# Entry into attention: query operands made earlier, searches held back, masks ranked last

## The chip, the cores and the metric

The kernel runs on one core of a Trainium2 chip. The metric is the device time of one launch in microseconds (us), the median of several runs. Five engines work in parallel, each through its own queue in order: TensorE (PE, the matrix multiplier; its weight loads are PEld), VectorE (DVE), ScalarE (ACT), GpSimd (POOL) and SyncE (SP), which here issues the loads and stores (DMA). An instruction that waits for an operand holds everything behind it on its engine. Matrix products go to PSUM, a small memory with eight banks; the rest lies in SBUF. The clock of TensorE is granted by a throttle and falls to half in some stretches; the profile shows it.

## What is computed

A decoder layer over 1024 tokens of width 1024. One projection of `h` gives queries, keys and values of 8 heads, the operands of a light indexer, and 512 pooling channels. The indexer scores every earlier token for every query; only the 256 best take part in the attention of that query. Then come an output projection, a layer norm and a gated feed-forward block with a second norm. What matters here:

```python
logits = einsum('bqhd,bsd->bqhs', iqb, ik) * (IDX_DIM ** -0.5)
score = einsum('bqh,bqhs->bqs', w, relu(logits))
score = where(causal, score, -inf)
_, idx = top_k(score, k_sel)              # k_sel = 256
...
s = einsum('bqhd,bqkhd->bhqk', qb, kg) * (HEAD_DIM ** -0.5)
p = softmax(where(valid, s, -inf))
o = einsum('bhqk,bqkhd->bqhd', p, vg)
```

## The kernel before, in words

**Tiles.** Tokens are cut into eight tiles of 128, numbered 0 to 7. Tile `i` sees `i + 1` tiles of keys, so tile 7 has scores of 128 x 1024 and tile 2 of 128 x 384. Tiles 0 and 1 see 256 tokens or fewer and need no selection. Matrix products are done in three passes of high and low parts, so an operand is a pair: ScalarE makes the high part by a copy and VectorE the low part by a subtraction.

**Searches and masks.** The 256th best score of each query is found by bisection on the bits of the score (`bisect`, lines 560 to 658): some first steps, 15 rounds over the upper half word, a middle step, 16 rounds over the lower one, then the mask, which overwrites the scores with a bias. A round counts with one instruction per tile how many scores lie above a candidate and updates the candidate with two short ones. Tiles 3 and the pair 5, 4 count on ScalarE (`TILES_A`, in `search_a`); tile 2 and the pair 7, 6 count on VectorE (`TILES_V`, in `search_v`). First steps, middle steps and masks of all of them run on VectorE. In the profile the search of 7 and 6 writes `junk_X` from `keysD_T`, that of 2 `junk_X` from `keysA_X` with `colsE_X`, that of 5 and 4 `junkA_T`, that of 3 `junkB_X`; `score_X` holds scores and, later, the masks.

**The planner.** While the program is written down, each queue (`Queue`, lines 131 to 183) keeps a modelled time with modelled costs (`cost`). Each search is a generator, a stream, that yields its next piece as (engine, cost) before it issues it. Whenever an instruction is about to be written and its operands are ready only later by the model, `fill` (line 693) is called: it looks for stream pieces of the same engine whose start plus cost fits before that time (with a small slack) and writes them first. Among those that fit it takes the one with the earliest start and, in a tie, one of ScalarE's streams (`st[3] not in TILES_A`); among equals the first in the list `streams` wins. The stream of tile 2 (`LATE`) gets nothing while the stream of 7 and 6 is unfinished. `need(i)` (line 689) writes all pieces that are left until the mask of tile `i` is issued. Where a queue's name is in `pinned`, the order written down is kept; elsewhere a scheduler may move independent instructions. `advance` pins the first piece of the stream of tile 2.

**Projections.** Lines 917 to 962 go over 24 groups `n_`: eight for the pooling channels, eight for keys (`k`, tile t), eight for values (`v`, tile t, groups 16 to 23). Work that follows a group, such as rotating and transposing a key tile (`k_transpose`) or taking a value tile into SBUF (`v_take`), is registered with `at_(slot, f)` and written behind the products of group `slot`. The queues of TensorE, VectorE, ScalarE and GpSimd are pinned here (and SP's).

**The entry.** Rotated queries lie in memory (`q_d`). Behind the last group, the queries of tiles 7 and 6 are loaded (`q_load`) and transposed by TensorE (`q_transpose`, four instructions each); what is left of the slots' work follows; then `q_make` writes `q_operands` for both: four ScalarE copies and two VectorE subtractions each. The operand of tile 7 lies in `qabh`, on the place of `hT`, that of tile 6 in `qabw[0]`, on the place of the projection weights `ws`, so neither can be written while the projections run.

**Attention.** 32 units, one for each group of two tiles `g` (3 first), pair of heads `pr` and tile `i`: tiles 7 and 6 alternate over four pairs, then 5 and 4, 3 and 2, 1 and 0. A unit has two score matrices (`u_scores`, tile `s`; PSUM holds those of one large unit at a time), the sum with the mask and the row maximum on VectorE, the exponential on ScalarE (`u_exp`, which calls `need(i)`), the division on GpSimd (`u_norm`), transposes on TensorE (`u_trans`, tile `pT`), and behind two tiles the product with the values (`pair_pv`, tile `o`) and its split (`pair_cat`). Scores run `AHEAD = 2` units ahead of the transposes. `Q_AT` places the query operands of the next group. Behind the last unit follow the output projection `wo` and the rest of the layer.

Of the kernel before, what the change touches and what calls it, by code (L numbers as in the profile page):

```python
# [12 lines left out]
F32R = mybir.dt.float32r  # L13
# [31 lines left out]
LATE = [2]  # L45
# [141 lines left out]
def decoder_layer_kernel(  # L187
# [84 lines left out]
    def raw_slot():  # L272
        n_raw[0] += 1
        return RAW[(n_raw[0] - 1) % 3]
# [280 lines left out]
    keys = {2: kA[:, 0:192], 3: kA[:, 192:448], 4: k4, 5: k5, 6: kD[:, 0:448], 7: kD[:, 448:960]}  # L555
    keys = {i: kw.bitcast(I16) for i, kw in keys.items()}

    biased = set()

    def bisect(tiles, cols, on_act):  # L560

# [9 lines left out]
        one = lambda c, m: c[:, m : m + 1]  # L571
        w_ = lambda i: (i + 1) / 8
        for m, i in enumerate(tiles):
            yield "V", 1.13 * w_(i)
            V.tensor_scalar(trash(i), score(i), 0.0, 0.0, ALU.is_ge, ALU.add, accum_out=one(cntc, m))
        yield "V", 0.6
        V.tensor_scalar(pr, cntc, float(TOPK), None, ALU.is_ge)
        V.tensor_scalar(sg, pr, 2.0, -1.0, ALU.mult, ALU.add)
        V.tensor_scalar(flip, pr, 32768.0, -32768.0, ALU.mult, ALU.add)
# [1 line left out]
            n = P * (i + 1)  # L581
            V.tensor_scalar(one(kp, m), one(pr, m), -float(2 * TOPK - 1 - n), -float(n - TOPK + 1), ALU.mult, ALU.add)
        for m, i in enumerate(tiles):
            yield "V", 1.1 * w_(i)

            hv = score(i).bitcast(I16).rearrange("p (n two) -> p n two", two=2)
            V.tensor_tensor(kv[i], hv[:, :, 1], one(flip, m).to_broadcast([P, P * (i + 1)]), ALU.bitwise_xor)
            if on_act:
                V.tensor_scalar(one(thr, m), one(kp, m), 2.0, float(P * (i + 1) + 1), ALU.mult, ALU.add)
        sum_w = sum(w_(i) for i in tiles)  # L590

        def search_v(bits, base, low):
            V.memset(cand, float(1 << (bits - 1)))
            for b in range(bits - 1, -1, -1):
                yield "V", 0.4 + 1.08 * sum_w + 0.35 * nt
                for m, i in enumerate(tiles):
                    dt = U16 if low else I16
                    V.tensor_scalar(trash(i).bitcast(dt), kv[i].bitcast(dt), one(cand, m), one(base, m),
                                    ALU.is_ge, ALU.add, accum_out=one(cntc, m))
                off = -float(1 << (b - 1)) if b > 0 else -1.0  # L600
                for m in range(nt):
                    V.tensor_scalar(one(pr, m), one(cntc, m), 0.0, float(1 << b), ALU.is_ge, ALU.mult)
                for m in range(nt):
                    V.tensor_scalar(one(cand, m), one(pr, m), one(cand, m), off, ALU.add, ALU.add)

        def search_a(bits, low):

            V.memset(cand, 0.5 - float(1 << (bits - 1)))
            for b in range(bits - 1, -1, -1):
                for m, i in enumerate(tiles):  # L610
                    yield "A", 0.9 * w_(i) + 0.45
                    A.activation(trash(i), kv[i].bitcast(U16 if low else I16), AF.Sign, bias=one(cand, m),
                                 accum_out=one(cntc, m))
                yield "A", 0.55 * nt

                for m in range(nt):
                    A.activation(one(pr, m), one(cntc, m), AF.Sign, bias=one(thr, m))
                for m in range(nt):
                    A.activation(one(cand, m), one(pr, m), AF.Identity, scale=-0.5 * float(1 << b), bias=one(cand, m))
            yield "V", 0.1  # L620
            V.tensor_scalar(cand, cand, -1.0, None, ALU.mult)

        yield from (search_a(15, False) if on_act else search_v(15, kp, False))
        V.tensor_copy(M, cand)
        for m, i in enumerate(tiles):
            yield "V", 1.8 * w_(i)
            V.tensor_scalar(trash(i).bitcast(I16), kv[i], one(M, m), one(kp, m), ALU.is_gt, ALU.add,
                            accum_out=one(ng, m))
            lv = score(i).bitcast(U16).rearrange("p (n two) -> p n two", two=2)
            V.scalar_tensor_tensor(kv[i].bitcast(U16), kv[i], one(M, m), lv[:, :, 0], ALU.is_equal, ALU.mult)  # L630
            if on_act:
                V.tensor_scalar(one(thr, m), one(ng, m), 2.0, float(P * (i + 1) + 1), ALU.mult, ALU.add)
# [31 lines left out]
    def open_stream(*a):  # L664
        pinned.update(PIN)
        b = bisect(*a)
        streams.insert(0, [T.t, next(b), b, a[0], True])
        times.fill = fill

    def start(st):  # L670
        return max(st[0], queues[st[1][0]].t)

    def advance(st):
        fill, times.fill = times.fill, None
        q = queues[st[1][0]]
        held = st[3] == LATE and st[4] and "V" not in pinned
        st[4] = False
        if held:
            pinned.add("V")
        try:  # L680
            st[1] = next(st[2])
        except StopIteration:
            streams.remove(st)
        st[0] = q.t
        if held:
            pinned.discard("V")
        times.fill = fill

    def need(i):
# [3 lines left out]
    def fill(q, until):  # L693
        while True:

            first = [st for st in streams if 7 in st[3]]
            todo = [st for st in streams if not (first and st[3] == LATE) and st[1][0] == q.name and start(st) + st[1][1] <= until + SLACK.get(q.name, 0.0)]
            if not todo:
                return
            advance(min(todo, key=lambda st: (start(st), st[3] not in TILES_A)))  # L700


    n_rr = [0]
# [209 lines left out]
    def take(t, pp, slot):  # L913
        raw = rope_pool(t, pp)
        at_(slot, lambda: k_transpose(t, raw))

    groups = [("u", g, c) for g in (3, 2, 1, 0) for c in range(2)] + [("k", t, 0) for t in range(NT)] + [("v", t, 0) for t in range(NT)]

    PAIRS = (0, 6, 8, 14, 16)
    held, pair = {}, None  # L920
    for n_, (kind, a, b) in enumerate(groups):
        if n_ in PAIRS:
            pb = psB("pair")
            held[n_], held[n_ + 1] = pb[:, 0:512], pb[:, 512:1024]
            pair = [(held[q_], u_f(*groups[q_][1:]) if kind == "u" else t_f(groups[q_][1])) for q_ in (n_, n_ + 1)]
        if n_ in held:
            for kp in range(2):
                for pp, f in pair:
                    f(pp, [4 * (n_ not in PAIRS) + 2 * kp, 4 * (n_ not in PAIRS) + 2 * kp + 1])
        else:  # L930
            held[n_] = psA("pj")
            (u_f(a, b) if kind == "u" else t_f(a))(held[n_], range(KT))
        pp = held[n_]
        if n_ in (2, 10):
            w_loads(wk_in if n_ == 2 else wv_in)
        if n_ in (7, 8, 15, 16):
            for kp in ((0, 1) if n_ % 2 else (2, 3)):
                w_split(kp)
        nd = n_ + 2 if n_ in PAIRS else n_ + 1
        if kind == "u":  # L940
            at_(nd, lambda a=a, b=b, pp=pp: u_take(a, b, pp))
            if b == 1:
                at_(nd + 1, lambda a=a: u_split(a))
                at_(nd + 1, lambda a=a: u_split2(a))
                at_(nd + POOL_AT, lambda a=a: u_pool(a))
        elif kind == "k":
            tr = n_ + (4 if n_ in PAIRS or n_ - 1 in PAIRS else 3)
            at_(nd, lambda a=a, pp=pp, tr=tr: take(a, pp, tr))
        else:
            at_(nd, lambda a=a, pp=pp: v_take(a, pp))  # L950
        if n_ == 20:
            SP.dma_start(GR, gate_d[0].to_broadcast([P, 1024]))
        q_ = n_ - MOD_AT
        if 0 <= q_ < 9:
            if q_:
                mod_fin(q_ - 1)
            if q_ < 8:
                mod_half(2 * q_)
        for f in late.pop(n_, []):
            f()  # L960
        if 0 <= q_ < 8:
            mod_half(2 * q_ + 1)
# [11 lines left out]

    ptb = [[buf("H", (2 * s_ + e) * 2048, 2048, "pT").rearrange("p (j q) -> p j q", j=8) for e in (0, 1)] for s_ in (0, 1)]
    smr = buf("H", 8192, 6144, "sm")
    qabh = buf("H", 14336, 1536, "qab", F32R)
    qabw = [buf("W", 2048 * i, 1536, "qab", F32R) for i in (0, 1)]
    qabx = [buf("X", 5312 + i * 1536, 1536, "qab", F32R) for i in (0, 1)]
    qab = {7: qabh, 6: qabw[0], 5: qabw[1], 4: qabw[0], 3: qabh, 2: qabx[0], 1: qabx[1], 0: qabh}  # L980

    qops = {}

    def q_load(i):
        raw = raw_slot()[:, 0:512]
        SP.dma_start(raw, q_d[i])
        return raw

    def q_make(i, raw, pt=None):
        b = qab[i]  # L990
        qops[i] = (b[:, 0:1024], b[:, 1024:1536])
        q_operands(pt if pt is not None else q_transpose(raw), *qops[i])

    for s_ in (last, last + 1):
        if s_ == last:
            qr = {i: q_load(i) for i in (7, 6)}
            qp = {i: q_transpose(qr[i]) for i in (7, 6)}
        for f in late.pop(s_, []):
            f()
    assert not late, late  # L1000
    for i in (7, 6):
        q_make(i, qr[i], qp[i])

    def cat_slot(g):
        return WS[g]

# [104 lines left out]
    for u in units[0:AHEAD]:  # L1111
        u_scores(u)
        u_exp(u)
    u_norm(units[0])
    nxt, nrm = AHEAD, 1
    for n_, u in enumerate(units):
# [760 lines left out]
```

## Time and profile before

| | |
|---|---|
| median of three runs | 1292.34 us (1291.21 to 1293.01) |
| the profiled execution | 1293.41 us |
| its span, first to last instruction | 1291.6 us |
| mean granted clock of TensorE | 0.972 |
| busy: PE, PEld | 1200.3 us (93%), 932.2 us (72%) |
| busy: DVE, ACT, POOL | 994.8 us (77%), 654.5 us (51%), 722.5 us (56%) |
| key and value projections end, attention follows | about 349 us |
| output projection follows attention | about 507 us |

A profile row of a timeline reads: start, duration (of the group, where several are merged), engine, operation, tile written <- tiles read, shape, count, and in brackets the idle time of the engine before it with the work that ended it. Tile names carry the letter of their place in SBUF (`score_X`, `qab_H`). A row of the windows gives, for a stretch from A to B, each engine's busy time with its count of instructions, then the granted clock (1.00 is full), the share of the DMA engines and GB/s. All helper calls have the same line, so instructions are told apart by their tiles.

### The profile page before, as it was taken

How to read it: one execution, taken by the hardware profiler on the slowest of the kernel's cores; microseconds unless marked ns; L12 is line 12 of the kernel's file. 1: busy time of each engine (PE TensorE's matmuls, PEld its weight loads, DVE VectorE, ACT ScalarE, POOL GpSimd, SP SyncE). 2: the span in 40 equal slices, each digit the busy share in tenths (PEclk: the TensorE clock that was granted, in tenths of full speed). 3: DMA queues.
4: the chain of work that ended last, by engine and by line, in shares of the span. 5: the costliest groups of instructions: out<-in, count | busy, mean ns of one | idle time of the engine just before them, and what ended most of it. 6: DMA issues, size and time to landing. Idle time of an engine off the chain costs nothing.

```text
span 1291.6 us, 16411 instructions
## 1 busy us (share of the span) xinstructions
PE 1200.3 (93%) x5622; PEld 932.2 (72%) x5622; DVE 994.8 (77%) x1845; ACT 654.5 (51%) x1343; POOL 722.5 (56%) x510
## 2 busy tenths in 40 slices
PE   7979999999879999997799999999999999999996
PEld 6656565687646666886678787878888787878775
DVE  6758998877979866568687778687877777687798
ACT  3346878797668687265443333343433333333531
POOL 1383375657012355267666657483847566576848
PEclk9989999999958999999899999999999999999998
DMA  9510048521000016300111021201121110203112
GB/s 350 200 72 17 10 159 321 196 82 57 17 1 17 9 50 214 129 9 9 65 66 66 33 82 34 82 33 66 33 65 39 60 66 33 90 33 107 49 66 114
DMA packets 32460, 103.40 MB, mean 80 GB/s; under 512 B 3573, under 2 KB 3573, under 8 KB 28793
## 3 DMA queue, kind: packets, MB, share of 16 engines
q1 hardware_dynamic: 32376, 102.36, 22.5%
q8 instruction: 44, 0.72, 0.2%
q14 instruction: 40, 0.32, 0.1%
HBM read 92.90 MB, written 9.45 MB: 79 GB/s over the span
## 4 chain that ended last, share of the span: by engine, by line
PE 60%; DVE 18%; POOL 9%; issue 7%; ACT 5%; DMA 1%; SPq 0%; DVEq 0%; POOLq 0%; ACTq 0%
PE gu L174 24%; PE dn L174 14%; PE pj L174 5%; PE wo L174 4%; PE pair L174 3%; PE s L174 2%; PE pT L174 2%; PE o L174 2%; DVE act_W L174 2%; DVE score_X L174 2%; POOL wraw_R L174 2%; DVE junk_X L174 2%; PE lg L174 2%; DVE utmp_X L174 1%; POOL ws_W L174 1%
## 5 line engine op out<-in xcount | busy, mean ns | idle before, releaser
L174 PE MATMUL gu<-hr_H,wblk_T 128*128 128x512 f32 (+1 forms) x924 | 217.5, 388 | 6.1 <-ACT gtmp_V L174 2.7
L174 PE MATMUL gu<-hr_H,wblk_V 128*128 128x512 f32 (+1 forms) x924 | 215.8, 385 | 4.3 <-POOL wblk_V L174 2.1
L174 PEld LDWEIGHTS gu<-hr_H,wblk_T 128*128 128x128 f32 x924 | 172.2, 191 | 42.4 <-POOL wblk_T L174 3.6
L174 PEld LDWEIGHTS gu<-hr_H,wblk_V 128*128 128x128 f32 x924 | 169.9, 188 | 41.4 <-POOL wblk_V L174 4.2
L174 DVE TENSOR_TENSOR res_X<-res_X,dn 128x512 f32<-128x512 f32 (+1 forms) x253 | 159.0, 679 | 15.4 <-PE dn L174 15.3
L174 PE MATMUL pj<-ws_W,hT_H 128*128 128x512 f32 x456 | 117.3, 406 | 8.8 <-POOL ws_W L174 6.7
L174 POOL TENSOR_TENSOR wraw_R<-wraw_R 128x512 f32<-128x512 f32 x64 | 94.6, 1486 | 47.0 <-DVE wblk_T L174 23.7
L174 POOL TENSOR_TENSOR wraw_W<-wraw_W 128x512 f32<-128x512 f32 x60 | 86.9, 1456 | 59.6 <-DVE wblk_V L174 29.3
L174 POOL TENSOR_SCALAR sm_H<-sm_H,stat_X 128x1024 f32<-128x1024 f32 (+7 forms) x64 | 48.0, 764 | 124.1 <-DVE stat_X L174 96.0
L174 PEld LDWEIGHTS pj<-ws_W,hT_H 128*128 128x128 f32 x456 | 85.0, 192 | 33.2 <-POOL ws_W L174 7.0
L174 PE MATMUL dn<-wblk_T,act_W 128*128 128x512 f32 x324 | 78.8, 391 | 4.3 <-DVE act_W L174 4.3
L174 PE MATMUL dn<-wblk_V,act_W 128*128 128x512 f32 x324 | 78.5, 391 | 2.9 <-DVE act_W L174 2.5
L174 DVE TENSOR_SCALAR_CACHE_REDUCE junk_X<-keysD_T,colsD_X 128x1024 int16<-128x1024 int16 (+1 forms) x64 | 78.9, 1268 | 0.2
L174 ACT ACTIVATE wblk_V<-wraw_R 128x512 fp32r<-128x512 f32 x56 | 35.2, 629 | 81.2 <-POOL wraw_R L174 62.7
L174 POOL TENSOR_TENSOR ws_W<-raw_R,ws_W 128x1024 fp32r<-128x1024 f32 x17 | 44.3, 2625 | 53.4 <-ACT ws_W L174 53.4
L174 PEld LDWEIGHTS dn<-wblk_T,act_W 128*128 128x128 f32 x324 | 60.4, 188 | 18.9 <-DVE act_W L174 6.4
L174 PEld LDWEIGHTS dn<-wblk_V,act_W 128*128 128x128 f32 x324 | 60.4, 188 | 17.4 <-DVE act_W L174 4.2
L174 ACT ACTIVATE wblk_V<-wraw_W 128x512 fp32r<-128x512 f32 x53 | 33.1, 627 | 75.0 <-POOL wraw_W L174 56.4
L174 ACT ACTIVATE wblk_T<-wraw_W 128x512 fp32r<-128x512 f32 x56 | 35.0, 628 | 65.9 <-POOL wraw_W L174 50.2
L174 ACT ACTIVATE wblk_T<-wraw_R 128x512 fp32r<-128x512 f32 x52 | 32.5, 627 | 60.5 <-POOL wraw_R L174 44.5
L174 ACT ACTIVATE utmp_X<-gu 128x512 f32<-128x512 f32 x33 | 19.7, 598 | 74.7 <-PE gu L174 74.7
L174 ACT ACTIVATE sm_H<-sm_H,stat_X 128x1024 f32<-128x1024 f32 (+7 forms) x64 | 49.1, 771 | 16.7 <-DVE stat_X L174 16.5
(295 smaller groups left out, 2763.7 us busy)
## 6 DMA issues: line engine op xcount, KB each, us to landing
mset_K<-in_wmr_dram SPq DMA_DIRECT2D x16, 1024.0 KB, 5.6
wm_K<-in_wma_dram SPq DMA_DIRECT2D x16, 512.0 KB, 10.0
wraw_R<-in_wg_dram SPq DMA_DIRECT2D x6, 1024.0 KB, 4.8
wraw_R<-in_wd_dram SPq DMA_DIRECT2D x12, 512.0 KB, 3.7
wraw_W<-in_wup_dram SPq DMA_DIRECT2D x12, 512.0 KB, 3.7
wraw_R<-in_wup_dram SPq DMA_DIRECT2D x10, 512.0 KB, 3.6
wraw_W<-in_wg_dram SPq DMA_DIRECT2D x5, 1024.0 KB, 4.9
wraw_W<-in_wd_dram SPq DMA_DIRECT2D x10, 512.0 KB, 3.5
```

The lines of the kernel that those rows point to most:

```text
L174: ins_ = f(*a, **k)
```

## The change

Four things are changed:

1. The query operands of tiles 7 and 6 get places of their own (`qabv`, in the area V behind the values), are loaded in group 17 and made in slots 20 and 21, that is, behind the products of value tiles 4 and 5.
2. A list `hold` is filled ahead of the last value group and emptied when units 0 and 1 of attention are issued. While it is filled, `fill` writes no piece on ScalarE and, on VectorE, only pieces of the stream with tile 7. When it is emptied, the next piece of each stream is pinned on its queue.
3. A tie between pieces goes no longer to all pieces of ScalarE's streams but to those that yield a third value: first and middle steps of ScalarE's searches. Masks have no such mark.
4. A round of a VectorE search is offered tile by tile, not whole.

```diff
-    biased = set()
+    biased, hold = set(), []
...
-            yield "V", 1.13 * w_(i)
+            yield "V", 1.13 * w_(i), on_act
             V.tensor_scalar(trash(i), score(i), 0.0, 0.0, ALU.is_ge, ALU.add, accum_out=one(cntc, m))
-        yield "V", 0.6
+        yield "V", 0.6, on_act
...
-            yield "V", 1.1 * w_(i)
+            yield "V", 1.1 * w_(i), on_act
...
             for b in range(bits - 1, -1, -1):
-                yield "V", 0.4 + 1.08 * sum_w + 0.35 * nt
                 for m, i in enumerate(tiles):
+                    yield "V", 0.3 + 1.08 * w_(i) + (0.35 * nt if m == nt - 1 else 0.0)
...
-            yield "V", 0.1
+            yield "V", 0.1, True
             V.tensor_scalar(cand, cand, -1.0, None, ALU.mult)
...
-            yield "V", 1.8 * w_(i)
+            yield "V", 1.8 * w_(i), on_act
             V.tensor_scalar(trash(i).bitcast(I16), kv[i], one(M, m), one(kp, m), ALU.is_gt, ALU.add,
...
-        streams.insert(0, [T.t, next(b), b, a[0], True])
+        streams.insert(0, [T.t, next(b), b, a[0], a[0] == LATE])
...
-        held = st[3] == LATE and st[4] and "V" not in pinned
+        held = st[4] and q.name not in pinned
...
-            todo = [st for st in streams if not (first and st[3] == LATE) and st[1][0] == q.name and start(st) + st[1][1] <= until + SLACK.get(q.name, 0.0)]
+            todo = [st for st in streams if not (first and st[3] == LATE) and not (hold and (q.name == "A" or 7 not in st[3])) and st[1][0] == q.name and start(st) + st[1][1] <= until + SLACK.get(q.name, 0.0)]
...
-            advance(min(todo, key=lambda st: (start(st), st[3] not in TILES_A)))
+            advance(min(todo, key=lambda st: (start(st), not (len(st[1]) > 2 and st[1][2]))))
...
+    qabv = [buf("V", 4096 + 1536 * i, 1536, "qab", F32R) for i in (0, 1)]
+    qab = {7: qabv[0], 6: qabv[1], 5: qabw[1], 4: qabw[0], 3: qabh, 2: qabx[0], 1: qabx[1], 0: qabh}
...
     for n_, (kind, a, b) in enumerate(groups):
+        if n_ == len(groups) - 1:
+            hold.append(1)
+        if n_ == 17:
+            qr.update((i, q_load(i)) for i in (7, 6))
+        if n_ in (20, 21):
+            at_(n_, lambda i=27 - n_: q_make(i, qr[i]))
...
     for s_ in (last, last + 1):
-        if s_ == last:
-            qr = {i: q_load(i) for i in (7, 6)}
-            qp = {i: q_transpose(qr[i]) for i in (7, 6)}
         for f in late.pop(s_, []):
             f()
-    for i in (7, 6):
-        q_make(i, qr[i], qp[i])
...
     for u in units[0:AHEAD]:
         u_scores(u)
         u_exp(u)
+    hold.clear()
+    for st in streams:
+        st[4] = True
```

More of the change, by code (lines that the diff above doesn't have):

```diff
@@ L589, in bisect @@
                 V.tensor_scalar(one(thr, m), one(kp, m), 2.0, float(P * (i + 1) + 1), ALU.mult, ALU.add)
-        sum_w = sum(w_(i) for i in tiles)
         def search_v(bits, base, low):
@@ L675, in advance @@
         q = queues[st[1][0]]
-        held = st[3] == LATE and st[4] and "V" not in pinned
+        held = st[4] and q.name not in pinned
         st[4] = False
         if held:
-            pinned.add("V")
+            pinned.add(q.name)
         try:
@@ L685, in advance @@
         if held:
-            pinned.discard("V")
+            pinned.discard(q.name)
         times.fill = fill
@@ L915, in take, with q_load, q_make @@
         at_(slot, lambda: k_transpose(t, raw))
+    qabh = buf("H", 14336, 1536, "qab", F32R)
+    qabw = [buf("W", 2048 * i, 1536, "qab", F32R) for i in (0, 1)]
+    qabx = [buf("X", 5312 + i * 1536, 1536, "qab", F32R) for i in (0, 1)]
+    qabv = [buf("V", 4096 + 1536 * i, 1536, "qab", F32R) for i in (0, 1)]
+    qab = {7: qabv[0], 6: qabv[1], 5: qabw[1], 4: qabw[0], 3: qabh, 2: qabx[0], 1: qabx[1], 0: qabh}
+    qops = {}
+    def q_load(i):
+        raw = raw_slot()[:, 0:512]
+        SP.dma_start(raw, q_d[i])
+        return raw
+    def q_make(i, raw, pt=None):
+        b = qab[i]
+        qops[i] = (b[:, 0:1024], b[:, 1024:1536])
+        q_operands(pt if pt is not None else q_transpose(raw), *qops[i])
     groups = [("u", g, c) for g in (3, 2, 1, 0) for c in range(2)] + [("k", t, 0) for t in range(NT)] + [("v", t, 0) for t in range(NT)]
@@ L920, in decoder_layer_kernel @@
     held, pair = {}, None
+    qr = {}
     for n_, (kind, a, b) in enumerate(groups):
+        if n_ == len(groups) - 1:
[4 more added lines that the diff above has]
+            at_(n_, lambda i=27 - n_: q_make(i, qr[i]))
         if n_ in PAIRS:
@@ L976, in decoder_layer_kernel @@
     smr = buf("H", 8192, 6144, "sm")
[L977 to L992, printed above, removed]
     for s_ in (last, last + 1):
-        if s_ == last:
-            qr = {i: q_load(i) for i in (7, 6)}
-            qp = {i: q_transpose(qr[i]) for i in (7, 6)}
         for f in late.pop(s_, []):
```

## The prediction

> **What bounds the kernel now.** I read the page first, its strip of the granted clock, then the table of windows around the dip, who TensorE waits for, and the timelines of the engines from 340 to 470 us.
>
> ```profile
> span 1291.6 us, 16411 instructions
> ...
> PEclk9989999999958999999899999999999999999998
> ```
>
> The clock is near full except in slices 12 and 13, from 355 us on: there attention begins. In the windows the columns are PE, PEld, DVE, ACT, POOL busy, then the clock.
>
> ```profile
> 300.00:343.00 43.00, 41.06 (x179) 33.77 (x180) 37.70 (x93) 28.40 (x73) 16.67 (x10) 0.96 0.14 43
> 343.00:349.50 6.50, 6.50 (x33) 5.26 (x32) 6.50 (x15) 4.80 (x13) 0.00 (x0) 1.00 0.00 1
> 349.50:364.30 14.80, 2.11 (x6) 1.16 (x5) 13.78 (x50) 13.88 (x33) 0.00 (x0) 0.67 0.12 35
> 364.30:376.20 11.90, 10.75 (x21) 5.02 (x21) 7.90 (x15) 5.60 (x9) 2.21 (x2) 0.50 0.00 1
> 376.20:443.00 66.80, 61.26 (x368) 42.52 (x369) 61.80 (x192) 49.68 (x114) 20.70 (x21) 0.91 0.03 9
> 443.00:466.00 23.00, 22.83 (x164) 15.41 (x163) 12.26 (x32) 19.50 (x46) 11.14 (x13) 1.00 0.10 36
> ```
>
> TensorE is full until 349.5, then works 2.11 of 14.80 us while VectorE and ScalarE are full, then runs at half clock. From 376 to 443 both TensorE and VectorE are over 90% busy; from 443 to 466 VectorE is idle 10.7 us. Who TensorE waits for from 343 to 507 us, and its timeline:
>
> ```profile
> PE s L174 <- ACT qab_H L174: 8.8, 1, 8.8
> PE s L174 <- DVE qab_H L174: 3.9, 1, 3.9
> ...
> 348.49 1.03 PE L174 MATMUL qT<-const_C,raw_R 128*128 128x128 f32 x8
> 358.28 2.08 PE L174 MATMUL s<-kr_K,qab_H 128*128 128x512 f32 x4 [8.76 <-ACT qab_H L174]
> 371.57 4.67 PE L174 MATMUL s<-kr_K,qab_H 128*128 128x512 f32 x8
> 376.17 3.67 PE L174 MATMUL pT<-const_C,sm_H 128*128 128x128 f32 x16
> 399.05 2.46 PE L174 MATMUL s<-kr_K,qab_H 128*128 128x512 f32 x8
> ```
>
> The transposes of the queries end at 349.5; the first scores wait 8.8 us for ScalarE's copy of the query operand and 3.9 us for VectorE's low part. What stood ahead of these two:
>
> ```profile
> 355.97 0.57 ACT L174 ACTIVATE vf_V<-pj 128x512 f32<-128x512 f32 x1
> 356.45 2.40 ACT L174 ACTIVATE qab_H<-qT 64x512 fp32r<-64x512 f32 x4
> 358.87 2.41 ACT L174 ACTIVATE qab_W<-qT 64x512 fp32r<-64x512 f32 x4
> ...
> 344.34 0.68 DVE L174 TENSOR_SCALAR score_X<-junk_X 128x1024 f32<-128x1024 bf16 x1
> 353.60 0.67 DVE L174 TENSOR_SCALAR_CACHE_REDUCE junk_X<-keysA_X,colsE_X 128x384 int16<-128x384 int16 x1
> 362.83 0.67 DVE L174 TENSOR_SCALAR_CACHE_REDUCE junk_X<-keysA_X,colsE_X 128x384 int16<-128x384 int16 x1
> 363.55 1.41 DVE L174 TENSOR_TENSOR qab_H<-qT,qab_H 64x512 fp32r<-64x512 f32 x2
> ```
>
> ScalarE took the last value tile only at 355.97, behind rounds of tile 3's search. VectorE ran rounds of tile 2's search, nine of them (the group row below), until 363.55. Both searches are wanted much later, and the mask of tile 7 (344.34) was there. So the hole is made by the order, and no engine's total work makes it.
>
> **The change, part by part.**
>
> *Operands of tiles 7 and 6 in the value projections.* The eight transposes (1.03 us) move ahead of the last projections; TensorE's sum is unchanged, so projections and transposes still end at 349.5. Slot by slot:
>
> ```profile
> 326.59 22.06 PE L174 MATMUL pj<-ws_W,hT_H 128*128 128x512 f32 x96
> ```
>
> These are four value tiles of 5.5 us; tile 7's operand is made behind the first of them, tile 6's behind the second. ScalarE's 2.40 + 2.41 us so go to about 332 to 341, where it works 28.40 of 43.00 us; VectorE's 2 x 1.41 us go there too, where it works 37.70 of 43.00. TensorE doesn't wait for either there, since the projections need only free PSUM, so I cost both at nothing; uncovered they would be 4.8 and 2.8 us. The two loads pass SP's queue earlier, and were early already:
>
> ```profile
> 304.26 5.00 SPq L168 DMA_DIRECT2D raw_R<-q_d  x3
> ```
>
> *The hold.* From the last value projection until units 0 and 1 are issued no round of tiles 3 and 2, and no mask of 5 and 4, may stand in the queues. The scores of unit 0 then follow the projections at once. The chain from there, with these rows:
>
> ```profile
> 365.54 1.22 DVE L174 CUSTOM_DVE_ANT_0 sm_H<-s,score_X 128x1024 f32<-128x1024 f32 x1 [0.59 <-PE s L174]
> 369.28 1.09 DVE L174 CUSTOM_DVE_ANT_0 sm_H<-s,score_X 128x896 f32<-128x896 f32 x1
> 366.81 1.15 ACT L174 ACTIVATE sm_H<-sm_H,stat_X 128x1024 f32<-128x1024 f32 x1 [2.87 <-DVE stat_X L174]
> 373.03 2.21 POOL L174 TENSOR_SCALAR sm_H<-sm_H,stat_X 128x1024 f32<-128x1024 f32 x2 [55.97 <-DVE stat_X L174]
> ```
>
> Scores of unit 0 at full clock, 2.46 (the 399.05 row): 349.5 to 352.0. VectorE takes the halves, 1.22 each: 353.2 and 354.4. Exponentials of 1.15 end near 355.8, GpSimd's 2.21 near 358.2. Unit 1's scores need the two PSUM halves that VectorE frees at 353.2 and 354.4, so end near 355.7; its halves leave at 356.8 and 357.9; the third unit's scores need those and end near 359.2. They stand ahead of the first pT transposes in program order. So pT starts at 359.2 in place of 376.17: **-17.0 us**. TensorE idles about 2.3 us in that stretch, in holes up to 1.3 us.
>
> *The clock.* Columns: busy, instructions, clock.
>
> ```profile
> 354.00:355.00 1.00, 0.00 (x0) 0.75 0.00 0
> 381.00:382.00 1.00, 1.00 (x6) 0.60 0.00 0
> 386.00:387.00 1.00, 0.08 (x1) 1.00 0.00 0
> 389.00:390.00 1.00, 1.00 (x6) 0.50 0.04 8
> 391.00:392.00 1.00, 1.00 (x7) 0.50 0.00 0
> ```
>
> The clock was half from about 354.5 to 381.6, so also for the 5.4 us behind 376.17, which at full clock need 2.7: that comes back. But about a microsecond of idleness near 386 was enough for another short stretch at half, the 389 to 391 rows; 3 to 4 us of it cost 1.7. I expect one such stretch in the new entry: 1.7 - 2.7 = **-1.0 us**, with ends of -2.7 (none) and +8.8 (half until 382 as before, 23 us of it in place of 5.4). I take the value by the 389 row, since no hole is as long as the old one.
>
> [...]
>
> *What is given back.* The rounds that filled the hole must run elsewhere.
>
> ```profile
> L174 DVE TENSOR_SCALAR_CACHE_REDUCE junk_X<-keysA_X,colsE_X 128x384 int16<-128x384 int16 x9 | 6.0, 672 | 0.3
> ...
> L174 DVE TENSOR_SCALAR_CACHE_REDUCE junk_X<-keysA_X,colsE_X 128x384 int16<-128x384 int16 x16 | 10.8, 672 | 0.4
> L174 DVE TENSOR_SCALAR_CACHE_REDUCE junk_X<-keysA_X,colsE_X 128x384 uint16<-128x384 uint16 x16 | 10.7, 669 | 0.2
> ...
> 440.83 0.35 DVE L174 TENSOR_SCALAR score_X<-junk_X 128x384 f32<-128x384 bf16 x1
> 466.08 0.56 DVE L174 CUSTOM_DVE_ANT_0 sm_H<-s,score_X 128x384 f32<-128x384 f32 x1 [1.15 <-PE s L174]
> ```
>
> A round's pitch is (362.83 - 353.60) / 8 = 1.15 us, nine are 10.4, and with the search's first steps 11.6 us (352 to 363.55) move behind the entry. Tile 2's mask was done at 441.2 and first read at 466.08, so there are 25 us of slack; VectorE idles 5.0 us in 376 to 443 and 10.7 in 443 to 466, 15.7 in all, and the moved operands leave 2.8 more. It fits, but barely: at the pace of 376 to 443, 23 rounds in 66.8 us, 32 rounds take 93 us; from 357.9 that is 451, where the first read, 16 us sooner, stands at 450. Attention stays in the stretch where TensorE idles 8% (5.54 of 66.80) for some 15 us longer, 1.2 us, and I add as much again for the last rounds: **+2.5 us**, with ends of 0 and 11.6.
>
> *Pieces by tile, and the ranking.* A round of tiles 7 and 6 can now be split in two, and the masks of 5 and 4 stand behind theirs.
>
> ```profile
> 310.78 1.39 DVE L174 TENSOR_TENSOR kr_K<-kT,kr_K 64x512 fp32r<-64x512 f32 x2 [3.16 <-ACT kr_K L174]
> 332.60:350.95 18.35, 6.56 (x8) 1.00 0.05 11
> ```
>
> Holes such as the 3.16 us ahead of 310.78 can take a half round; each filled one brings the masks forward. If few are filled, the masks of 5 and 4 (the second row, at least 6.56 us of VectorE in eight instructions) fall behind the hold. I take nothing for either and keep 6.6 us for a rival.
>
> Sum: -17.0 - 1.0 + 2.5 = -15.5. The later stages are shifted whole: they wait for nothing but attention and loads in program order. The profiled execution took 1293.41 us; its span is 1291.6 with 1.8 around it; 1293.41 - 15.5 = 1277.9. The median of the runs lies 1.07 under the profiled one, so **1276.8 us**.
>
> **The rivals.**
> *VectorE is the bound.* Both the 11.6 us and the 6.6 us of masks land in a stretch where it is 93% busy (61.80 of 66.80); against 15.7 spare, a third to a half comes back as TensorE's waits, 7 to 8 us in place of 2.5: about 1282. For it: the row of 376 to 443. Against: 10.7 us idle just behind, and 25 us of slack.
> *Clock held, holes filled.* No stretch at half (1.7 better) and nothing given back (2.5 better): -19.7, about 1272.6. Against: the 389 row. [...]
> *Slower.* The place is the first unit of tile 2, near 450: whatever rounds are left when it is issued run in one block with TensorE idle. Each costs 1.15 us; 14 left over eat the 15.5 us, and 20 give 23 us, +8 or about 1300. For it: the finer pieces are offered only where the planner sees a gap long enough. Against: it placed 23 in 66.8 us before.
> *It doesn't do what it says.* The operands are in the queues at the new slots, but ScalarE still reaches them late behind rounds of tile 3 ordered ahead: the wait stays and so does the time, 1292. Against: 8 us lie between 341 and the end of the projections.
>
> **How the numbers follow.** Forecast 0.50; VectorE bound 0.20; clock held 0.17; slower 0.07; no effect 0.06. Faster by over 0.2%, which is 2.6 us and about what a measurement of this kernel tells from no change, are the first three, 0.87; the same 0.06; slower 0.07. The range goes from 1270, a little under the held clock, to 1287, where 5 us are left of the gain, and leaves out the last two cases and some edges.
>
> **What the changed profile would show.** Right: qab copies before 343 on ScalarE, scores within a microsecond of the last projection, the first pT near 359, no 27 us stretch of clock 0.5. The given-back part shows as tile 2's mask ending less than 10 us ahead of its first read. Wrong: a wait of the first scores on VectorE's mask of tile 7, or a block of tile 2's rounds with TensorE idle before its first unit.

## The result, and the profile after

| | before | after |
|---|---|---|
| median (runs) | 1292.67 us (4: 1291.21 to 1293.72) | 1283.54 us (4: 1281.36 to 1284.73) |
| profiled execution, its span | 1293.41, 1291.6 us | 1283.98, 1282.2 us |
| first `pT` transposes | 376.17 us | 359.14 us |
| transposes of tile 3's query | 448.83 us | 440.56 us |
| first `wo` product | 502.71 us | 494.41 us |

The change makes the kernel faster: ratio 0.9928, 95% interval [0.9911, 0.9945], 9.1 us. The forecast was 15.5. Of the difference between the two profiled spans, 9.4 us, 8.3 are there at the first `wo` product, and the other 1.1 lie behind attention. The page of after, its first line and the strip of the granted clock:

```profile
span 1282.2 us, 16414 instructions
...
PEclk9989999999988999998899999999999999999998
```

The deep dip in slice 12 (0.5 before) is gone, but slices 12 and 13 still show 0.8. First the entry. TensorE's timeline of after:

```profile
348.56 1.73 PE L174 MATMUL s<-kr_K,qab_V 128*128 128x512 f32 x8
351.71 7.50 PE L174 MATMUL s<-kr_K,qab_V 128*128 128x512 f32 x16 [1.41 <-DVE stat_X L174]
359.14 3.67 PE L174 MATMUL pT<-const_C,sm_H 128*128 128x128 f32 x16
...
383.04 0.66 PE L174 MATMUL qT<-const_C,raw_R 128*128 128x128 f32 x4 [0.29 <-DVE colsE_X L174]
...
401.92 0.66 PE L174 MATMUL qT<-const_C,raw_R 128*128 128x128 f32 x4
...
412.35 0.90 PE L174 MATMUL s<-kr_K,qab_W 64*128 64x512 f32 x2 [4.00 <-DVE qab_W L174]
...
440.56 0.65 PE L174 MATMUL qT<-const_C,raw_R 128*128 128x128 f32 x4
```

The first scores follow the projections without a wait; one hole of 1.41 us is left in the entry, and the first `pT` starts 17.03 us sooner. The three `qT` rows are the query transposes of tiles 5, 4 and 3; they stand at fixed places in the order of the units, so they serve as milestones for the rest. The query operands on ScalarE, then on VectorE with the mask of tile 7:

```profile
333.23 2.39 ACT L174 ACTIVATE qab_V<-qT 64x512 fp32r<-64x512 f32 x4
340.68 2.40 ACT L174 ACTIVATE qab_V<-qT 64x512 fp32r<-64x512 f32 x4
```

```profile
324.79 0.69 DVE L174 TENSOR_SCALAR score_X<-junk_X 128x1024 f32<-128x1024 bf16 x1
338.19 1.39 DVE L174 TENSOR_TENSOR qab_V<-qT,qab_V 64x512 fp32r<-64x512 f32 x2
345.44 1.39 DVE L174 TENSOR_TENSOR qab_V<-qT,qab_V 64x512 fp32r<-64x512 f32 x2
```

Both operands are ready before the projections end, and the mask of tile 7 stands 19.5 us earlier than in the kernel before (344.34 there).

Now where the gain went. The windows between milestones, before and then after; the columns are length, PE, PEld, DVE, ACT, POOL busy, then the clock. The rows are the entry, then from the first `pT` to the query of tile 5, to that of tile 4, to that of tile 3, and to the first `wo`:

```profile
349.52:376.17 26.65, 12.82 (x26) 6.15 (x25) 21.66 (x64) 19.42 (x42) 2.21 (x2) 0.59 0.07 20
376.17:398.70 22.53, 21.32 (x118) 15.49 (x118) 18.96 (x61) 16.28 (x42) 8.44 (x8) 0.80 0.00 1
398.70:416.81 18.11, 15.55 (x88) 10.47 (x86) 17.34 (x53) 15.52 (x36) 4.21 (x4) 0.91 0.06 16
416.81:448.83 32.02, 30.22 (x211) 20.84 (x210) 27.64 (x86) 21.43 (x46) 10.70 (x12) 1.00 0.04 9
448.83:502.71 53.88, 51.88 (x366) 35.18 (x367) 35.26 (x119) 49.18 (x133) 32.49 (x39) 1.00 0.35 123
```

```profile
348.56:359.14 10.58, 9.17 (x26) 4.25 (x24) 7.97 (x15) 7.96 (x13) 1.70 (x2) 0.73 0.01 2
359.14:383.04 23.90, 23.15 (x125) 15.47 (x124) 22.53 (x72) 19.84 (x51) 9.41 (x9) 0.90 0.00 1
383.04:401.92 18.88, 15.85 (x82) 10.81 (x82) 17.55 (x58) 16.60 (x44) 4.21 (x4) 0.82 0.05 15
401.92:440.56 38.64, 33.94 (x207) 23.14 (x207) 33.42 (x111) 23.15 (x53) 11.08 (x12) 0.87 0.03 8
440.56:494.41 53.85, 51.83 (x366) 35.16 (x367) 35.10 (x119) 49.13 (x133) 32.56 (x39) 1.00 0.36 122
```

Behind the first `pT` the stretches are longer by 1.37, 0.77, 6.62 and -0.03 us: 8.7 of the 17.0 us are given back, three quarters of it between the queries of tiles 4 and 3. VectorE is busy 73.50 us in the middle three, 63.94 before: 9.6 us more. Nine more rounds of tile 2 stand there, those that ran in the old hole, 9.8 us by their rows. The end of tile 4's mask, which fell behind the hold, stands there too, three rows of 1.31, 0.48 and 0.48 us; some other rows are shorter, or overlap. VectorE is idle 7.9 us in the three (81.42 - 73.50), and 8.7 before: almost the same. Whom TensorE waits for after, from 343 to 507 us:

```profile
PE s L174 <- DVE stat_X L174: 4.2, 6, 1.4
PE s L174 <- DVE qab_W L174: 4.0, 1, 4.0
PE o L174 <- ACT pT_H L174: 1.0, 1, 1.0
```

The longest wait, 4.0 us, is for the low part of tile 4's query operand. On VectorE eight rounds of tile 2 stood ahead of it, from 402.95 to 411.6 (the groups of 402.9 to 411.7), and only then the operand, though ScalarE's last copy had ended at 406.63:

```profile
L174 DVE TENSOR_SCALAR_CACHE_REDUCE junk_X<-keysA_X,colsE_X 128x384 uint16<-128x384 uint16 x8 | 5.4, 670 | 0.3
```

The clock by microseconds (busy, instructions, clock) shows how long it is at half behind the two holes:

```profile
353.00:354.00 1.00, 1.00 (x3) 0.75 0.00 0
363.00:364.00 1.00, 1.00 (x4) 0.63 0.00 0
...
411.00:412.00 1.00, 0.00 (x0) 0.77 0.00 0
421.00:422.00 1.00, 1.00 (x3) 0.61 0.00 0
```

After the hole of 1.41 us the clock is half for about ten microseconds (353.5 to 363.7), and again for ten behind the wait of 4.0. The rounds themselves end early: tile 2's mask is done at 438.71, 19 us ahead of its first read.

```profile
437.97 0.74 DVE L174 TENSOR_SCALAR score_X<-junk_X 128x384 f32<-128x384 bf16 x1
457.79 0.56 DVE L174 CUSTOM_DVE_ANT_0 sm_H<-s,score_X 128x384 f32<-128x384 f32 x1 [1.13 <-PE s L174]
```

### The profile page after: what moved, and what is told of

Same layout as the page of the kernel before. It is cut to its first block, busy times and chain, and to the rows that moved or that the text cites. A ratio compares the mean times of both kernels' runs of the same rounds, so it can differ in the third digit from the quotient of the medians.

```text
span 1282.2 us, 16414 instructions
## 1 busy us (share of the span) xinstructions
PE 1203.4 (94%) x5622; PEld 934.5 (73%) x5622; DVE 1000.0 (78%) x1845; ACT 653.1 (51%) x1343; POOL 722.5 (56%) x510
## 4 chain that ended last, share of the span: by engine, by line
PE 39%; DVE 7%; POOL 4%; issue 2%; ACT 1%; DVEq 0%; POOLq 0%; ACTq 0%
PE gu L174 24%; PE dn L174 14%; DVE act_W L174 2%; POOL wraw_R L174 1%; DVE utmp_X L174 1%; POOL wraw_W L174 1%; DVE gtmp_V L174 1%; POOL wblk_T L174 1%; DVE wblk_T L174 0%; DVE hr_H L174 0%; POOL hr_H L174 0%; DVE res_X L174 0%; DVE stat_C L174 0%; POOL wblk_V L174 0%; DVE wblk_V L174 0%
## 5 line engine op out<-in xcount | busy, mean ns | idle before, releaser
L174 ACT ACTIVATE junkA_T<-keys_T,colsA_X 128x768 bf16<-128x768 uint16 (+3 forms) x62 | 54.4, 877 | 3.8 <-DVE colsA_X L174 2.9
```

The costliest lines, as they stand in the source:

```text
L174: ins_ = f(*a, **k)
```

## The experiments

The theories. A: the entry needs both the earlier operands and the hold; what was given back is one block, the eight rounds ahead of tile 4's operand, with the half clock behind it. B: VectorE's total of search work sets the end of attention, whatever its order. Later, C: the block is the fault of the order in which VectorE's instructions are built. Beside these runs the kernel before took 1291.91 us (for the first four), 1292.56 (the next four), 1293.14 (three) and 1292.33 (the last); each ratio is to the one beside it.

**Parts of the change alone.** The first has the earlier operands, but no hold, the old tie and whole rounds:

```diff
-            hold.append(1)
+            pass
...
-    hold.clear()
-    for st in streams:
-        st[4] = True
```

> Only the operands of tiles 7 and 6 are moved; no hold, the old tie rule, rounds whole. Theory A (the entry needs both, and the part given back comes from one block of tile 2's rounds ahead of a later operand): the first scores follow the projections, but rounds of tile 2 and 3 stand ahead of VectorE's first halves and of the last value tile, so the first pT comes 6 to 12 us sooner than before and not 17; about 1285 us. Theory B (VectorE's total of searches sets the end of attention, whatever the order): the rounds run in the hole as before, so nothing is owed later, and the time is that of the changed kernel or better, 1281 to 1284.

1288.79 us, ratio 0.9975 [0.9966, 0.9983]. TensorE:

```profile
350.50 1.73 PE L174 MATMUL s<-kr_K,qab_V 128*128 128x512 f32 x8
358.01 10.90 PE L174 MATMUL s<-kr_K,qab_V 128*128 128x512 f32 x20 [5.78 <-DVE stat_X L174]
368.84 3.67 PE L174 MATMUL pT<-const_C,sm_H 128*128 128x128 f32 x16
```

The operands are there, but the first pass over the scores waits for tile 7's mask, which VectorE ends at 356.49 here:

```profile
355.80 0.69 DVE L174 TENSOR_SCALAR score_X<-junk_X 128x1024 f32<-128x1024 bf16 x1
```

The masks of tiles 5 and 4 stand ahead of it, which the old tie puts first, and no round of tile 2 or 3 stands between the projections and this mask on VectorE. So the first `pT` comes 7.3 us sooner than before, within theory A's 6 to 12, but not for the reason that it gave. The time misses both theories' numbers. The second has the hold alone, with the operands where they were (old tie and whole rounds here too):

```diff
-        if n_ == 17:
-            qr.update((i, q_load(i)) for i in (7, 6))
-        if n_ in (20, 21):
-            at_(n_, lambda i=27 - n_: q_make(i, qr[i]))
...
+    for i in (7, 6):
+        q_make(i, qr[i], qp[i])
```

> Only the hold; operands are made behind the projections as before, the old tie rule, rounds whole. Theory A: ScalarE's copies (2.4 us) and VectorE's low part (1.4 us) stand between projections and first scores, some 4 us, and the clock falls in that hole; the first pT 12 to 14 us sooner than before, the same debt of rounds; about 1287 us. Theory B: as the changed kernel, 1283 to 1285, since the hole is short against the debt.

1290.83 us, ratio 0.9987 [0.9978, 0.9997]. The first `pT` starts at 363.38, 12.8 us sooner than before, as theory A had it, and yet only about 1 us of time is won: both theories' times are missed. An early entry alone is worth little; what counts is what stands behind it. Next, the change with whole rounds again, and the change with the old tie:

```diff
-                for m, i in enumerate(tiles):
-                    yield "V", 0.3 + 1.08 * w_(i) + (0.35 * nt if m == nt - 1 else 0.0)
+                yield "V", 0.4 + 1.08 * sum(w_(i) for i in tiles) + 0.35 * nt
+                for m, i in enumerate(tiles):
```

> The changed kernel with rounds offered whole again. Theory A: fewer holes ahead of 343 us are filled, so tile 7's mask comes some 10 us later (still in time) and the masks of 5 and 4 fall behind the hold, 5 us more debt: 1285 to 1288. But a whole round of tile 2 is planned at 1.155 us, its real length, and the split one at 1.055, so the block in front of tile 4's operand may be shorter by one or two rounds: then no change, 1283. Theory B: 5 us more debt, 1288.

```diff
-            advance(min(todo, key=lambda st: (start(st), not (len(st[1]) > 2 and st[1][2]))))
+            advance(min(todo, key=lambda st: (start(st), st[3] not in TILES_A)))
```

> The changed kernel with the old tie rule (masks of ScalarE's tiles before those of 7 and 6). Theory A: tile 7's mask is still done before the first scores, so the entry is unchanged and the masks of 5 and 4 are done before the hold: the same time, 1282 to 1285. Theory B: less is owed behind the hold, some 3 us better, 1280.

1286.57 us, 0.9957 [0.9944, 0.997], and 1287.48 us, 0.9961 [0.9946, 0.9975]: each part is worth some 3 to 4 us of the change, but both intervals touch or nearly touch that of the change, so the size is loose. With whole rounds the first `pT` starts at 359.20, as in the change; tile 7's mask ends 10.4 us later, at 335.85, and the masks of 5 and 4 fall behind the hold, as theory A expected, and the time is in its range. From the first `pT` to the first `wo` VectorE then has 7.5 us more to do than in the change (116.13 against 108.60), and the first `wo` comes 2.0 us later: 6.3 us of VectorE's work, with the last two rounds and the mask of tile 2, run behind tile 3's query here, in a stretch that is 2.3 us longer (56.14 against 53.85).

With the old tie the masks of 5 and 4 are done ahead of the hold, VectorE has 0.5 us less to do than in the change (108.07), and both theories are missed: the first `pT` starts at 361.20, the first `wo` at 500.91. The seven runs spread widely, and with the granted clock: from 1283.36 us at a mean clock of 0.978 to 1290.31 at 0.967, which is the profiled one.

**The block.** No piece of a search is written on VectorE while the query operands of tiles 5 and lower are written:

```diff
-            if not todo:
+            if not todo or (quiet and q.name == "V"):
                 return
...
+            quiet.append(1)
             q_make(t, q_load(t))
+            quiet.clear()
```

> The changed kernel, and while the operands of tiles 5 and below are written no search piece may be put on VectorE's queue. Theory A (the loss is the block of eight rounds ahead of tile 4's low part: a wait of 4.0 us and about 10 us of half clock behind it): the wait and that stretch go, the rounds fit later, 4 to 9 us better, 1275 to 1279. Theory B (VectorE's total decides): the rounds stand ahead of something else that TensorE needs, 1282 to 1285.

1285.78 us, 0.995 [0.9937, 0.9964]. The wait is still there, with the same eight rounds ahead of it:

```profile
412.86 0.90 PE L174 MATMUL s<-kr_K,qab_W 64*128 64x512 f32 x2 [4.10 <-DVE qab_W L174]
```

So the edit doesn't take the block away, and the run tests neither theory. The reason is in the code: `pinned` is emptied ahead of attention, so the order written there is not binding on VectorE, and this edit changed only the order written.

**The clock in the entry.** Six extra products stand between the scores of units 0 and 1; their results are not read. They fill the hole of 1.41 us:

```diff
         u_scores(u)
         u_exp(u)
+        if u == units[0]:
+            keep = psA("keep")
+            for _ in range(6):
+                T.matmul(keep, qops[7][0][:, 0:P], kst[:, 0, 0:512], start=True, stop=True)
```

> The changed kernel with six extra products of 512 columns between the scores of units 0 and 1, into a PSUM bank that nobody reads, to fill the hole of 1.4 us. Theory A: if that hole is what sends the clock to half at 353, the clock stays full until 363 and the first pT starts some 2 us sooner, with 2 us more from the half clock behind it: 1279 to 1281. Theory B: the scores wait for VectorE's halves anyway, the time is unchanged, 1283. If the clock still falls, the hole is not the cause, and the time is 1283 too.

1283.45 us, 0.9936 [0.9923, 0.9948]: the time of the change, as theory B had it. The clock in the entry's microseconds:

```profile
353.00:354.00 1.00, 1.00 (x4) 1.00 0.08 16
...
361.00:362.00 1.00, 1.00 (x5) 0.50 0.00 0
```

The ten microseconds at half clock are gone; about three are left around 361, and between 348 and 440 us half clock falls from 27.3 to 20.5. The first `pT` comes 1.4 us sooner, at 357.72, but tile 3's transposes only 1.3 us and the first `wo` 0.8 us sooner, and of that nothing can be measured. With the edit of the quiet operands as well:

> Both edits of e5 and e6 in one kernel. Theory A: the gains add, 1273 to 1277. Theory B: 1282 to 1285.

1285.41 us, 0.9945 [0.9932, 0.9958]. The wait for tile 4's operand falls to 1.5 us here, but the block has not gone: the same eight rounds stand ahead of the low part, which starts at 412.26 (411.62 in the change). TensorE only comes to it later, after other waits (by the profile 1.9 us for tile 2's search on VectorE and 2.2 for GpSimd). So this run doesn't decide between block and total either.

**Less VectorE work.** The lower 16 rounds of tile 2's search are left out, 18.5 us of VectorE, so that tile 2's mask is not the reference's:

```diff
-        yield from (search_a(16, True) if on_act else search_v(16, ng, True))
+        if tiles != LATE:
+            yield from (search_a(16, True) if on_act else search_v(16, ng, True))
```

> The changed kernel without the lower 16 rounds of tile 2's search (18.5 us of VectorE work less; the mask of tile 2 is then not the reference's). Theory A: the block ahead of tile 4's operand is made of those rounds, so wait and half clock go: 1274 to 1277, close to what e5 reaches. Theory B: VectorE's whole debt is gone, and it comes out clearly below e5, 1268 to 1273.

1278.10 us, 0.9891 [0.9877, 0.9906], above both theories' ranges. The rounds that are left out are those of the block, so the run takes away block and total together. The same stretches as above, from the first `pT` on:

```profile
357.27:380.94 23.67, 21.58 (x124) 13.50 (x124) 22.90 (x73) 20.15 (x51) 9.96 (x9) 1.00 0.00 1
380.94:401.61 20.67, 17.25 (x83) 10.99 (x83) 18.53 (x53) 17.36 (x46) 4.93 (x4) 0.78 0.04 13
401.61:433.79 32.18, 31.45 (x207) 21.23 (x207) 19.46 (x50) 22.39 (x52) 10.68 (x12) 0.93 0.03 9
```

The stretch from tile 4's query to tile 3's takes 32.18 us: what it took before the change, 32.02. With no round in it or with seven (before) TensorE, busy 94 to 98% of it, sets its length; with twelve (after) it takes 38.64, and the five further rounds at 1.15 us are 5.8 us beside the 6.6. This fits, but doesn't prove it: with the wait of 4.0 us and the clock at 0.87 in place of 1.00, the same 6.6 us can be told from TensorE's side. The first stretch, whose 16 upper rounds are still run, keeps its length of after (23.67 against 23.90), with VectorE busy 97% of it. The clock in it is full here and 0.90 in the change; with the extra products it is 23.91 at 0.93, with both edits 23.68 at 1.00. So in this stretch VectorE sets the length, and a clock between 0.90 and 1.00 doesn't matter. A lower one seems to: with the old tie the stretch takes 27.93 us at 0.84, though VectorE is busy 22.48 of them.

**VectorE's order kept as written.** In the order written, tile 2's rounds stand at most three together. From the end of the hold until the searches are done VectorE is pinned to it:

```diff
     hold.clear()
+    pinned.add("V")
...
+        if not streams:
+            pinned.discard("V")
```

> The changed kernel with one thing more: from the end of the hold until the searches are done, VectorE's instructions stay in the order in which the code writes them (before, only the first piece of each search did, and the build was free to move the others). As written, tile 2's rounds stand at most three in a row and three stand ahead of the low part of tile 4's query operand; in the changed kernel's trace eight stand there. Theory C (the loss behind the entry is this block, and the block is the build's order, not the plan's): the wait of 4.0 us for that operand falls under 1 us and the half clock from 411 to 421 with it, so 4 us of waiting and about 5 us of half clock are won, less 2 us that come back as short waits elsewhere: 1275 to 1279 us. Theory B (VectorE's total of search work sets the end of attention, whatever its order): the waits change places and the time stays at 1282 to 1285 us. Lost with the kept order would be time where the written order is worse than the build's (a pass that waits in order behind a row not yet made): 1286 or more.

> The kept order, and the six extra products on TensorE between the scores of the first two units, which kept the clock full through the entry before (the products' results are not read). Theory C: with VectorE's order mended, a faster entry is no longer eaten by the block, so this is 1 to 2 us below the kept order alone: 1273 to 1278 us. Theory B: like the changed kernel, 1282 to 1285 us.

> The kernel before, with VectorE's order kept as written from the first unit's normalization until the searches are done, and nothing else. In its trace the entry's 16 us hole gave the rounds their time, and only 1.8 us were waited for tile 4's operand. Theory C: the written order mends little here, 0 to 3 us: 1289 to 1293 us, so that the order matters because the change moved the entry and left the rounds where they were. If it gains 6 us or more, the order was a loss of the kernel before as well and is no price of this change. Theory B: no difference.

1296.96 us, 1.0037 [1.0025, 1.0049]; with the extra products of the entry 1297.23, 1.0034 [1.0022, 1.0046]; the kernel before with the order kept 1296.17, 1.0028 [1.0017, 1.0039]. All three are slower than the kernel before: theory C falls in this form, and so does theory B's "whatever its order". It is the case of a written order that is worse than the build's. In the first of them VectorE stood at one instruction:

```profile
396.60 1.23 DVE L174 CUSTOM_DVE_ANT_0 sm_H<-s,score_X 128x1024 f32<-128x1024 f32 x1
...
406.77 0.15 DVE L174 TENSOR_SCALAR colsA_X<-colsA_X 128x1 f32<-128x1 f32 x1 [8.94 <-ACT colsA_X L174]
```

That is tile 3's search, which waits for ScalarE; in a kept order everything behind it waits too. So one more run writes that piece later:

```diff
-            todo = [st for st in streams if not (first and st[3] == LATE) and not (hold
+            todo = [st for st in streams if not (first and st[3] == LATE) and not (wait3 and st[3] == [3] and q.name == "V") and not (hold
...
+        if u[0] < 3:
+            wait3.clear()
```

> The changed kernel with VectorE's order kept as written, as in the run that took 1296.96 us, and with VectorE's closing pieces of tile 3's search written only once the units of the second group begin. In that run VectorE stood 8.94 us, from 397.83 to 406.77, at the first of these pieces, which waited in order for ScalarE's search to end, and the wait for tile 4's operand was 0.2 us instead of 4.0. Theory C (the order of the rounds is the loss behind the entry): without that stop, no block of more than three rounds and no wait over 1.5 us is left between 360 and 440, and the time comes to 1276 to 1281 us. Theory B (VectorE's total of work behind the entry sets the time, and the order only says where it shows): the waits are spread over more, shorter ones, and the time is 1282 to 1286 us. If an order that is kept costs by itself, in many waits of less than 1 us, it is over 1287.

1288.72 us, 0.9969 [0.9957, 0.9982]. No wait of TensorE is over 1.5 us from 343 to 507, and that for tile 4's operand is gone. The stretches:

```profile
359.76:386.04 26.28, 24.98 (x116) 16.07 (x117) 22.23 (x70) 19.53 (x49) 7.73 (x8) 0.76 0.00 1
386.04:403.35 17.31, 14.46 (x82) 8.52 (x83) 16.52 (x53) 16.25 (x42) 4.25 (x5) 1.00 0.05 17
403.35:446.30 42.95, 40.47 (x220) 24.75 (x220) 38.93 (x121) 26.64 (x60) 13.10 (x15) 0.88 0.02 7
```

The first stretch, at a clock of 0.76, takes 2.4 us more than in the change, with VectorE busy 0.3 less. Without the block the third stretch is 42.95 us, longer than the 38.64 with it; VectorE is busy 38.93 of them. Over the three it is idle 8.9 us, as it was before and after. The expectation of theory C (1276 to 1281) is missed by 8 us. The time lies above theory B's 1282 to 1286 as well, in the case of a kept order that costs by itself: VectorE is busy 4.2 us longer in this order than in the change (77.69 against 73.50), 1.3 us of it one more pass over scores within the stretch, so the run does not hold the total fixed.

The stretch from the first `pT` to tile 3's query in the runs that bear on it, from windows over exactly that stretch:

| kernel | length, us | DVE busy | DVE idle | first `wo` |
|---|---|---|---|---|
| before | 72.66 | 63.95 | 8.7 | 502.71 |
| operands alone | 75.06 | 66.64 | 8.4 | 498.55 |
| after | 81.42 | 73.50 | 7.9 | 494.41 |
| quiet operands | 81.00 | 73.13 | 7.9 | 495.30 |
| extra products | 81.57 | 73.88 | 7.7 | 493.60 |
| hold alone | 82.52 | 77.38 | 5.1 | 499.95 |
| kept order, tile 3 later | 86.54 | 77.69 | 8.9 | 499.39 |
| whole rounds | 81.09 | 74.69 | 6.4 | 496.43 |
| old tie | 85.85 | 72.94 | 12.9 | 500.91 |
| quiet operands and extra products | 81.63 | 73.81 | 7.8 | 495.03 |
| 16 rounds fewer | 76.52 | 60.89 | 15.6 | 488.42 |

Where all rounds are run, the length lies 5 to 9 us above VectorE's busy time in nine of these kernels. Outside stand the old tie (clock 0.83) and the other three with a kept order (12.2 to 19.0 idle). Where rounds are left out, VectorE has twice the idle time and no longer sets the length throughout.

## Why the prediction was right, and where it was not

**The entry: right.** Predicted was the first `pT` at 359.2, measured 359.14. That it came out to a tenth is luck, since details were off and cancelled: the projections ended 0.96 us sooner than assumed and unit 0's scores took 1.73 us in place of 2.46, while the clock was half from 353.5 on, which the chain had taken as full. Sixteen scores took 7.50 us so, and 5.14 at full clock in the run with fewer rounds. That the operands had to move is shown by the run with the hold alone: its first scores wait 1.5 us for ScalarE's copy, and its first `pT` comes 4.2 us later than in the change. That the hold is needed is not shown: the run with the operands alone lacks the new ranking and the split rounds too, and what it waited for was the mask of tile 7, the wait that the prediction named as a sign of being wrong. No run leaves out the hold and nothing else.

**Operands in the projections at no cost: right.** The copies stand at 333.23 and 340.68, no projection waits for them in after (one waits 1.2 us for a low part in the run with the operands alone). **Ranking and split rounds at nothing: probably too low.** Each alone measures some 3 to 4 us, with intervals that meet that of the change or nearly do. And the mask of tile 4 did fall behind the hold, which the prediction kept for a rival.

**The clock: wrong in size.** Predicted was -1.0 us, with one stretch of 3 to 4 us at half. There were about ten microseconds behind a hole of 1.41 us, six to seven around 398 and ten from 411. From the clock column of the middle three windows (a mean of 0.87 is 26% of the stretch at half clock), half clock lasts 21.6 us after and 12.3 before, so up to 4.6 us more of TensorE's time is lost. But the extra products took some 7 us of half clock out of the entry, and the time stayed. So in the entry the half clock is not what sets the end, nor, down to a mean of 0.90, in the first stretch behind it. Further on that is open.

In after the clock went to half behind 1.41 us of idleness (0.75 in the microsecond from 353, 0.50 from 354 on); so the case of the held clock, 1272.6 us, is refuted here. In the run with fewer rounds the same hole of 1.41 us (ahead of 350.82) left the clock full, at 1.00 from 350 to 355. What makes the difference is not shown.

**What is given back: the step that failed.** The prediction said of the moved rounds that VectorE "idles 5.0 us in 376 to 443 and 10.7 in 443 to 466, 15.7 in all", that "It fits, but barely", and took +2.5 us with ends of 0 and 11.6. Measured are 8.7 behind the first `pT`, with the half clock there in it, which the prediction had in another term; the rounds' share alone is not measured. The amount moved was right: nine rounds, and VectorE is busy 9.6 us more. The spare time was not spent. The idle time ahead of tile 3's query stayed (8.7 us before, 7.9 after, over the three stretches), and the 2.8 us that the moved operands were to leave were no spare either: they had stood in the entry, from 363.55 to 368.09, and not behind it. The pace of 23 rounds in 66.8 us was no limit: 32 rounds ran from 360.37 to 430.5, 70 us in place of 93. The 10.7 us behind 443 were not reached: the rounds were done early, so VectorE is as idle from 440.56 to 494.41 as it was (35.10 busy of 53.85), and tile 2's mask still ends 19 us ahead of its first read, where fewer than 10 were predicted. Slack at the end of a chain of work helps only if something puts the work there.

**The rival "VectorE is the bound"** gave 7 to 8 us back and about 1282; it had a chance of 0.20 and came nearest, to 1.5 us. The first stretch bears it out, as told above, and the run with 16 rounds fewer agrees: 5.4 us faster, with the last of the three stretches at its old length, though 1.9 us of that stood already at the first `pT`. As a rule for all of attention it is not shown. Theory B's own numbers were met by the extra products alone, and missed by less than 1 us with the quiet operands; with whole rounds 7.5 us more of VectorE's work cost 2.0 us, and with the old tie less work took longer. That the block of eight rounds is the loss is not supported either: in the last run it is gone, and the stretch is longer than with it; but that run has VectorE busy longer too. **The rival on the slow side** did not occur, since no round was left at tile 2's first unit.

A further rival was not tested: the half clock behind the query of tile 5. The half clock that came on top took up to 4.6 of the 8.7 us. The old tie speaks for it: at a clock of 0.83 in place of 0.87 its three stretches hold some 8 us more of half clock, worth up to 3.9 us, and they are 4.4 us longer with about the same work of VectorE; its runs go with the clock as well. So does the first stretch of the last run. Against it stands the hold alone, whose three stretches take 82.52 us at a clock of 0.90, where the operands alone have the same 0.90 and take 75.06. No run keeps the clock full there.

What stays open: how the 6.6 us between the queries of tiles 4 and 3 divide among VectorE's total, the block and the half clock; and whether rounds put behind 440 us by hand would bring what the shorter search brings, about 5 us. That was not tried; with whole rounds, where 6.3 us of work ended up there, they cost 2.3 us of length.

## What to carry to other kernels

When a hole is closed that another engine was using, ask what that engine did there and in which stretch it will do it now; if the next stretch has it as busy as here (61.80 of 66.80 us before), reckon with the moved work in full first, and count idle time as spare only where you can name what will put the work there. A part of a change that moves a wait is worth only what the stage behind it lets through: the hold brought the entry forward by 12.8 us and the kernel by 1. Before an order written down is blamed or tuned, see in the trace whether it is the order that runs.

## What the runs showed of the hardware

A hole of 1.41 us on TensorE, with work on both sides, was followed by ten microseconds at half clock in after (353.5 to 363.7) and by none in the run with fewer rounds; with 1.66 us of extra products in it the clock stood at 1.00 until 359. VectorE's operations on bf16 with two tensors, or on bf16 in and f32 out, took two durations in these traces: GpSimd worked from 357.44 to 360.11 us in after, and of two operations with 128x640 elements

```profile
359.13 1.31 DVE L174 TENSOR_TENSOR keys_T<-keys_T,score_X 128x640 bf16<-128x640 bf16 x1
...
360.96 0.48 DVE L174 TENSOR_TENSOR junkA_T<-junkA_T,keys_T 128x640 bf16<-128x640 bf16 x1
```

the one beside it took 1.31 us, and the same kind behind it 0.48. In the last run, with GpSimd busy from 358.52 to 361.03, the first of this pair started ahead of it and took 0.47; the second, beside it, took 1.29, and the one that writes f32 1.30 in place of 0.48. The rounds of tile 2's search show no such pair: they took 0.65 to 0.67 us in after, and the one at 363.76, with GpSimd busy from 363.34 to 365.34, took 0.66. Why the two kinds differ is not shown.
